# Fourteen matmul products of a feed-forward layer in another order, one weight piece ahead of another, and one token tile's split on another engine

## The chip, the cores and the metric

The kernel runs on one core of one Trainium2 chip. The metric is device time in microseconds (us) of one execution. Five engines work side by side, each through its own queue in the order of the program: TensorE (PE, matmuls), VectorE (DVE), ScalarE (ACT), GpSimd (POOL), and SyncE (SP), which here only issues DMAs.

## What is computed

One layer of a bidirectional hybrid backbone over 128 context tokens and 1024 latent tokens, 1152 in all, with a model width of 1024. The change touches the end of the mixer and the first product of the feed-forward part:

```python
out = (g_rg * y_rg + g_ml * y_ml) @ lw['w_out']          # output projection
...
x = layer_norm(ALPHA * x + gate1 * mix, lw['ln_g'][0], lw['ln_b'][0])
u = layer_norm(x) * (1.0 + scale2) + shift2
hid = jnp.square(jax.nn.relu(u @ lw['w_fc'] + lw['b_fc']))   # 1024 -> 4096
x = layer_norm(ALPHA * x + gate2 * (hid @ lw['w_proj'] + lw['b_proj']), ...)
```

## The kernel before

**Split operands.** Every fp32 operand is held as two parts, a rounded high part and the rest. `split` (lines 66 to 68) makes them: ACT copies the value to the high part (line 67), then another engine, DVE or POOL, subtracts (line 68). A product is three matmuls per 128 rows of the inner dimension, high by high, low by high and high by low (`mm3`, lines 111 to 113).

**Output projection (`wout`, `chain`, `chain2`, `cols`).** Nine token tiles `t` of 128 tokens are projected in turn. `chain(t)` adds the residual and normalises on DVE, ACT and POOL. `cols(t - 3)` transposes a tile on PE, scales it on ACT, writes its high part into `hi` on ACT (line 1070) and `u` to HBM (`u_d`, line 1071), and returns a function that writes the low part `lo` on DVE (line 1072). In the last pass, `t = 8`, that function (for tile 5) is called behind `chain(8)`. Then the first feed-forward products run, over columns of 384 tokens: with `c = 0` (tiles 0 to 2), then `c = 1` (tiles 3 to 5), with `chain2(7)`, `chain2(8)` and `cols(6)` to `cols(8)` between them.

**First feed-forward product (`ffn1`).** The 32 blocks of hidden columns go in 16 pairs `p`. The pairs 0 to 2 are computed plainly. Beside them DVE, ACT and POOL build sums of the inputs, `Th` and `Tl`, from `u_d` (`sums`, `t_loads`). The pairs 3 to 15 use Strassen's scheme in Winograd's form: seven products in place of eight, each for two halves `s` of the tokens, so fourteen products a pass, of 12 matmuls on 288 columns each. They are numbered 1 to 7 and use the weight pieces A11 (1), S1 (5), S2 (6), S3 (7), A12 (2), A22 (4) and S4 (3). The list `steps` sets their order. It names for each the product, the half, the PSUM bank (A, B or C, one of each per half), whether the bank is begun afresh, and what follows: `keep` copies the bank's present sum to SBUF on ACT (line 1297), and later products go on adding to that bank; `out` adds a bank and a kept copy on DVE (line 1306) and then applies the ReLU on ACT (line 1131), or the ReLU straight from the bank. `end` squares on DVE (line 1311).

Two things run between the steps. `need`, after every second step, makes one more weight piece for the next pass through the generator `prep`: a `put` (ACT's high part, then the low part on POOL or, for A12, on DVE) and one DVE sum (lines 1162 to 1171). Two pieces share a tile `w`, and there are four tiles. A pass has seven pieces, so pairs of pieces fall one way in the passes with odd `p` and another way with even `p`. A piece that begins a tile waits until every product that reads the two pieces eight back has ended. `pump`, after the other steps, makes one part of `store` for the pass before (sums of `hid` on POOL, lines 1105 to 1114, and DMAs). The last pass, 15, makes no new pieces and prepares `ffn2`.

Of the kernel before, what the change touches and what calls it, by code (L numbers as in the profile page):

```python
# [9 lines left out]
F = mybir.dt.float32  # L10
R = mybir.dt.float32r
AF = mybir.ActivationFunctionType
OP = mybir.AluOpType
# [6 lines left out]
NT = 9  # L20
C = 384
# [18 lines left out]
class Kern:  # L40
# [881 lines left out]
    def branches(self, st, hrp):  # L922
        nc, I, O = self.nc, self.I, self.O
# [16 lines left out]
        for br in range(2):  # L940
# [3 lines left out]
            for d, cs in [(0, (0,)), (1, (0,)), (0, (1,)), (1, (1,)), (0, (2,)), (1, (2,))] * (1 - br) + \  # L944
# [12 lines left out]
                w, g = pair[d]  # L957
# [45 lines left out]
        def chain(t, pss):  # L1003
            x = p3.tile([128, D], F, name="xr", tag="xr", bufs=2)
            nc.sync.dma_start(x, I["x"][t])
            y = p3.tile([128, D], F, name="y", tag="y", bufs=2)
            if t == 1:
                row("g1l", self.mod_d[0][1])
            g = rows["g1l" if t else "g1c"]
            for n in range(2):  # L1010
                nc.vector.tensor_tensor(y[:, n * 512:(n + 1) * 512], pss[n], g[:, n * 512:(n + 1) * 512], OP.mult)
            nc.vector.scalar_tensor_tensor(y, x, ALPHA, y, OP.mult, OP.add)
            mv = self.ln_stats(y)
            self.normalise(y, y, mv)
            e = nc.vector if t == NT - 1 else nc.gpsimd
            e.tensor_tensor(y, y, rows["gn"], OP.mult)
            e.tensor_tensor(y, y, rows["bn"], OP.add)
            ys[t] = y
# [9 lines left out]
        def wout(t):  # L1028
            c, o = t // 3, (t % 3) * 128
            pss = []  # L1030
            for n in range(2):
                ps = self.ps.tile([128, 512], F, name="wps", tag="xb", bufs=5)
                s = slice(n * 512, (n + 1) * 512)
                for k in range(KT):
                    self.mm3(ps, mh[c][0][:, k, o:o + 128], mh[c][1][:, k, o:o + 128], wo[k][:, 0, s], wo[k][:, 1, s],
                             k == 0, k == KT - 1)
                pss.append(ps)
            lo = cols(t - 3) if t >= 3 else None
            chain(t, pss)
            if t == NT - 1:  # L1040
                lo()
                return
            if t >= 1:
                chain2(t - 1)
            if lo:
                lo()

        def cols(t, bank=self.pj):
            c, o = t // 3, (t % 3) * 128
            if t % 3 == 0:  # L1050
                h, l = self.hilo(c)
                self.hi.append(h)
                self.lo.append(l)
            z = xn.pop(t)
            u = z.rearrange("p (k t) -> p k t", t=128)
            j = 1 if t else 0
            for g in range(2):
                tp = bank()
                for i in range(4):
                    k = 4 * g + i  # L1060
                    nc.tensor.transpose(tp[:, i * 128:(i + 1) * 128], z[:, k * 128:(k + 1) * 128], self.ident)
                for i in range(4):
                    k = 4 * g + i
                    q = tp[:, i * 128:(i + 1) * 128]
                    if t >= 6 and g == 1:
                        nc.vector.tensor_scalar(u[:, k, :], q, m2[:, 1, k, j:j + 1], m2[:, 0, k, j:j + 1], OP.mult, OP.add)
                    else:
                        nc.scalar.activation(u[:, k, :], q, AF.Identity, scale=m2[:, 1, k, j:j + 1], bias=m2[:, 0, k, j:j + 1])
            h, l = self.hi[c][:, :, o:o + 128], self.lo[c][:, :, o:o + 128]
            nc.scalar.activation(h, u, AF.Copy)  # L1070
            nc.scalar.dma_start(self.u_d[:, :, t * 128:(t + 1) * 128], u)
            return lambda: nc.vector.tensor_tensor(l, u, h.bitcast(F), OP.subtract)

        self.hi, self.lo = [], []
        for t in range(NT):
# [46 lines left out]
    def ffn1(self, st):  # L1122
# [22 lines left out]
        def put(x, e):  # L1145
            if pos[1] % 2 == 0:
                pos[0] = self.ring.tile([128, 2, 1024], R, name="w", tag="w", bufs=4)
            o = (pos[1] % 2) * 512
            w = pos[0][:, :, o:o + 512]
            pos[1] += 1  # L1150
            self.split(w[:, 0], w[:, 1], x, e)
            ready.append(w)

        def prep():
            for p in range(3, 16):
                r = raw.pop(p)
                a11, a12, a21, a22 = (r[i][:, 512 * k:512 * k + 512] for i in range(2) for k in range(2))
                t = lambda: pe.tile([128, 512], F, name="S", tag="S", bufs=5)
                v, g = nc.vector, nc.gpsimd
                s1, s2, s4 = t(), t(), t()  # L1160
                put(a11, g)
                v.tensor_tensor(s1, a21, a22, OP.add)
                yield
                put(s1, g)
                v.tensor_tensor(s2, s1, a11, OP.subtract)
                yield
                put(s2, g)
                v.tensor_tensor(a21, a11, a21, OP.subtract)
                yield
                put(a21, g)  # L1170
                v.tensor_tensor(s4, a12, s2, OP.subtract)
                yield
                put(a12, v)
                load(p + 1, 0)
                yield
                put(a22, g)
                load(p + 1, 1)
                yield
                put(s4, g)
                yield  # L1180
# [82 lines left out]
        for _ in work:  # L1263
            pass

        A = {"A11": 0, "S1": 1, "S2": 2, "S3": 3, "A12": 4, "A22": 5, "S4": 6}
        pair = lambda k, j: lambda s: (B(self.X[0], k, s, j), B(self.X[1], k, s, j))
        tt = lambda i: lambda s: tuple(a[:, i, :, HN * s:HN * s + HN] for a in (Th, Tl))
        P = {1: ("A11", pair(0, 0)), 5: ("S1", tt(0)), 6: ("S2", tt(1)), 7: ("S3", tt(2)),
# [9 lines left out]
        for p in range(3, 16):  # L1279
            H = new_h()  # L1280
            base = 7 * (p - 3)
            bank = {}
            ev = {}

            def mul(n, s, b, first):
                if first:
                    bank[b, s] = self.pj()
                ps = bank[b, s][:, :HN]
                w = ready[base + A[P[n][0]]]
                xh, xl = P[n][1](s)  # L1290
                for k in range(4):
                    ks = slice(k * 128, k * 128 + 128)
                    self.mm3(ps, w[:, 0, ks], w[:, 1, ks], xh[:, k, :], xl[:, k, :], first and k == 0, k == 3, not first)

            def keep(i, s):
                ev[i, s] = pe.tile([128, HN], F, name="e", tag="e", bufs=6)
                nc.scalar.activation(ev[i, s], bank["A", s][:, :HN], AF.Copy)  # L1297

            hb = lambda i, s, j: H[:, i, 2 * HN * s + HN * j:2 * HN * s + HN * j + HN]

            def out(i, s, j, b, e=None):
                o = hb(i, s, j)
                if e is None:
                    relu(o, bank[b, s][:, :HN], 2 * p + i)
                else:
                    nc.vector.tensor_tensor(o, bank[b, s][:, :HN], ev[e, s], OP.add)
                    relu(o, o, 2 * p + i)

            def end(s):
                q = H[:, :, 2 * HN * s:2 * HN * s + 2 * HN]  # L1310
                nc.vector.tensor_tensor(q, q, q, OP.mult)

            steps = [(1, 0, "A", True, lambda: keep(1, 0)), (1, 1, "A", True, lambda: keep(1, 1)),
                     (5, 0, "C", True, None), (6, 0, "A", False, lambda: keep(2, 0)),
                     (5, 1, "C", True, None), (6, 1, "A", False, lambda: keep(2, 1)),
                     (7, 0, "A", False, lambda: (keep(3, 0), out(1, 0, 1, "C", 3))),
                     (2, 0, "B", True, lambda: out(0, 0, 0, "B", 1)),
                     (7, 1, "A", False, lambda: (keep(3, 1), out(1, 1, 1, "C", 3))),
                     (4, 0, "A", False, lambda: out(1, 0, 0, "A")),
                     (2, 1, "B", True, lambda: out(0, 1, 0, "B", 1)),  # L1320
                     (3, 0, "C", False, lambda: (out(0, 0, 1, "C", 2), end(0))),
                     (4, 1, "A", False, lambda: out(1, 1, 0, "A")),
                     (3, 1, "C", False, lambda: (out(0, 1, 1, "C", 2), end(1)))]
            for i, (n, s, b, first, after) in enumerate(steps):
                mul(n, s, b, first)
                if after:
                    after()
                if i % 2:
                    need(base + 8 + i // 2 + 1)
                else:  # L1330
                    pump()
                if p == 15:
                    early(i)
            if p < 15:
                stores.append(store(p, H))
# [431 lines left out]
```

## Time and profile before

| | us |
|---|---|
| median of 3 runs | 2231.91 (2229.61 to 2234.83) |
| the profiled execution | 2234.51 |
| its span, from the first to the last instruction | 2232.4 |
| PE busy in it | 2112.8 (95%) |
| DVE, ACT, POOL busy | 1409.6, 994.9, 854.0 |

The profiled execution lies 2.6 us above the median and within the spread of the runs. 2.1 us of it lie outside the span. The stage that the change is about runs from some 1441 to 1824 us: the last tiles of the output projection to 1447, the plain pairs to 1522, the thirteen passes to 1823. In the rows of a timeline the first number is the start in us from the span's start, the second the duration in us, and the note in brackets the idle time of that engine just before and what ended it.

### The profile page before, as it was taken

The page shows a single profiled execution, that of the slowest core. Times are in us where ns is not written, and L with a number is a line of the kernel's source. Part 1 is how long each engine was busy: PE and PEld are TensorE (multiplying, and loading weights), DVE is VectorE, ACT ScalarE, POOL GpSimd, SP SyncE. Part 2 cuts the span into 40 slices and gives each one's busy share as a digit, 9 for nine tenths or more (in the row PEclk, how much of TensorE's full clock was granted, in tenths as well). Part 3 has the DMA queues.
Part 4 walks back from the last instruction along what each step waited for, and adds up shares of the span by engine and source line. Part 5 has one row for each costly group of instructions (what it writes and reads, how often), then busy time and mean ns, then how long its engine had stood idle before and what let it go on. Part 6 is the DMA issues. An engine that isn't in the chain of part 4 may idle for free. (4 is left out here: it accounts for less than half of the span.)

```text
span 2232.4 us, 31968 instructions
## 1 busy us (share of the span) xinstructions
PE 2112.8 (95%) x12507; PEld 1986.1 (89%) x12507; DVE 1409.6 (63%) x2248; ACT 994.9 (45%) x1634; POOL 854.0 (38%) x507
## 2 busy tenths in 40 slices
PE   7999999999999999999989999999999998999984
PEld 3889999999999989999989998899999996888863
DVE  4456776676675644888564656866454556566677
ACT  5455425414424525777721423655444443343333
POOL 1402213312421312332212214448566656466476
PEclk9999999999999999999989999999999999999997
DMA  7121241142122141110533333454343464342532
GB/s 275 38 71 50 66 146 64 54 133 86 62 87 83 53 77 46 48 48 29 165 120 128 118 117 115 131 199 136 125 143 121 147 245 158 136 170 79 204 118 108
DMA packets 116647, 251.13 MB, mean 112 GB/s; under 512 B 21332, under 2 KB 53716, under 8 KB 111888
## 3 DMA queue, kind: packets, MB, share of 16 engines
q1 hardware_dynamic: 94976, 231.19, 30.7%
q10 hardware_dynamic: 21520, 17.90, 2.4%
q8 instruction: 98, 1.61, 0.3%
q14 instruction: 53, 0.43, 0.1%
HBM read 186.38 MB, written 62.67 MB: 112 GB/s over the span
## 5 line engine op out<-in xcount | busy, mean ns | idle before, releaser
L111 PE MATMUL pj<-hi,w 128*128 128x384 f32 (+1 forms) x2144 | 712.8, 332 | 18.1 <-ACT XP L805 7.9
L112 PE MATMUL pj<-lo,w 128*128 128x384 f32 (+1 forms) x2144 | 709.8, 331 | 12.9 <-DVE lo L68 6.3
L113 PE MATMUL pj<-hi,w 128*128 128x384 f32 (+1 forms) x2144 | 709.2, 331 | 1.3 <-POOL w L68 1.1
L111 PEld LDWEIGHTS pj<-hi,w 128*128 128x128 f32 x2144 | 406.4, 190 | 20.3 <-ACT XP L805 8.2
L112 PEld LDWEIGHTS pj<-lo,w 128*128 128x128 f32 x2144 | 406.4, 190 | 15.4 <-DVE lo L68 6.9
L113 PEld LDWEIGHTS pj<-hi,w 128*128 128x128 f32 x2144 | 406.0, 189 | 1.9 <-POOL w L68 1.4
L68 POOL TENSOR_TENSOR w<-ws,w 128x512 fp32r<-128x512 f32 (+1 forms) x64 | 113.1, 1769 | 292.0 <-ACT w L67 283.8
L111 PE MATMUL pps<-w,hi 128*128 128x512 f32 x512 | 204.0, 398 | 11.3 <-ACT w L67 9.1
L112 PE MATMUL pps<-w,hi 128*128 128x512 f32 x512 | 204.0, 398 | 6.2 <-POOL w L68 4.1
L113 PE MATMUL pps<-w,lo 128*128 128x512 f32 x512 | 202.9, 396 | 1.4 <-DVE lo L68 1.4
L68 DVE TENSOR_TENSOR w<-ws,w 128x1024 fp32r<-128x1024 f32 (+1 forms) x85 | 112.7, 1334 | 122.6 <-ACT w L67 122.5
L67 ACT ACTIVATE w<-ws 128x1024 fp32r<-128x1024 f32 (+1 forms) x149 | 129.5, 878 | 80.8 <-PE pj L113 67.5
L467 POOL PARTITION_ALL_REDUCE aacc<-aacc x16 | 56.0, 3541 | 256.6 <-DVE aacc L466 256.6
L722 POOL TENSOR_TENSOR CS<-Cst,CS 128x516 fp32r<-128x516 f32 x56 | 73.8, 1319 | 158.2 <-ACT CS L721 147.7
L111 PE MATMUL pj<-Th,w 128*128 128x288 f32 x416 | 123.3, 296 | 8.0 <-ACT e L1297 8.0
L111 PEld LDWEIGHTS pps<-w,hi 128*128 128x128 f32 x512 | 98.0, 191 | 34.5 <-ACT w L67 10.4
L112 PEld LDWEIGHTS pps<-w,hi 128*128 128x128 f32 x512 | 98.0, 191 | 29.7 <-POOL w L68 4.9
L113 PE MATMUL pj<-Th,w 128*128 128x288 f32 x416 | 122.6, 295 | 0.0
L112 PE MATMUL pj<-Tl,w 128*128 128x288 f32 x416 | 122.5, 295 | 0.0
L113 PEld LDWEIGHTS pps<-w,lo 128*128 128x128 f32 x512 | 98.1, 192 | 23.4 <-DVE lo L68 1.9
L68 POOL TENSOR_TENSOR lo<-lo,hi 128x1024 fp32r<-128x1024 f32 (+1 forms) x31 | 84.8, 2735 | 74.0 <-ACT hi L67 74.0
L67 ACT ACTIVATE w<-raw 128x512 fp32r<-128x512 f32 x88 | 50.9, 622 | 109.9 <-issue 62.8
(348 smaller groups left out, 4493.2 us busy)
## 6 DMA issues: line engine op xcount, KB each, us to landing
ws<-in_w_in SPq DMA_DIRECT2D x56, 512.0 KB
lo<-h_d SPq DMA_DIRECT2D x28, 1024.0 KB
aw<-in_w_ada SPq DMA_DIRECT2D x64, 256.0 KB
ws<-in_w_fc SPq DMA_DIRECT2D x32, 512.0 KB
h_d<-Hf SPq DMA_DIRECT2D x32, 512.0 KB
raw<-in_w_pr SPq DMA_DIRECT2D x32, 512.0 KB
h_d<-S SPq DMA_DIRECT2D x48, 256.0 KB
gm<-gs ACTq DMA_DIRECT2D x48, 192.0 KB
```

The costliest lines, as they stand in the source:

```text
L67: self.nc.scalar.activation(hi, x, AF.Copy)
L68: (eng or self.nc.vector).tensor_tensor(lo, x, hi.bitcast(F), OP.subtract)
L111: mm(out, lhsT=ah, rhs=bh, start=first, stop=False, skip_group_check=onto)
L112: mm(out, lhsT=ah, rhs=bl, start=False, stop=False, skip_group_check=onto)
L113: mm(out, lhsT=al, rhs=bh, start=False, stop=last, skip_group_check=onto)
L467: nc.gpsimd.partition_all_reduce(acc[j], acc[j], channels=128, reduce_op=ReduceOp.add)
L722: nc.gpsimd.tensor_tensor(CS[d][1], Cst[d], CS[d][0].bitcast(F), OP.subtract)
```

## The change

Four edits. The order of the fourteen products is another one; the piece A12 takes place 3 in a pass and S3 place 4, both where they are made and where they are looked up; the low part of token tile 5 is made on POOL; and in the last pass of the output projection it is issued ahead of `chain(8)` and not behind it.

```diff
             lo = cols(t - 3) if t >= 3 else None
+            if t == NT - 1:
+                lo()
             chain(t, pss)
             if t == NT - 1:
-                lo()
                 return
...
-            return lambda: nc.vector.tensor_tensor(l, u, h.bitcast(F), OP.subtract)
+            e = nc.gpsimd if t == 5 else nc.vector
+            return lambda: e.tensor_tensor(l, u, h.bitcast(F), OP.subtract)
...
-                put(a21, g)
+                put(a12, v)
                 v.tensor_tensor(s4, a12, s2, OP.subtract)
                 yield
-                put(a12, v)
+                put(a21, g)
                 load(p + 1, 0)
...
-        A = {"A11": 0, "S1": 1, "S2": 2, "S3": 3, "A12": 4, "A22": 5, "S4": 6}
+        A = {"A11": 0, "S1": 1, "S2": 2, "S3": 4, "A12": 3, "A22": 5, "S4": 6}
...
-                     (5, 0, "C", True, None), (6, 0, "A", False, lambda: keep(2, 0)),
-                     (5, 1, "C", True, None), (6, 1, "A", False, lambda: keep(2, 1)),
+                     (5, 0, "C", True, None), (5, 1, "C", True, None),
+                     (6, 0, "A", False, lambda: keep(2, 0)), (6, 1, "A", False, lambda: keep(2, 1)),
+                     (2, 0, "B", True, lambda: out(0, 0, 0, "B", 1)),
                      (7, 0, "A", False, lambda: (keep(3, 0), out(1, 0, 1, "C", 3))),
-                     (2, 0, "B", True, lambda: out(0, 0, 0, "B", 1)),
+                     (2, 1, "B", True, lambda: out(0, 1, 0, "B", 1)),
                      (7, 1, "A", False, lambda: (keep(3, 1), out(1, 1, 1, "C", 3))),
                      (4, 0, "A", False, lambda: out(1, 0, 0, "A")),
-                     (2, 1, "B", True, lambda: out(0, 1, 0, "B", 1)),
                      (3, 0, "C", False, lambda: (out(0, 0, 1, "C", 2), end(0))),
```

In tables, with a product written as number and half, the order of a pass is

```
before  1.0 1.1 5.0 6.0 5.1 6.1 7.0 2.0 7.1 4.0 2.1 3.0 4.1 3.1
after   1.0 1.1 5.0 5.1 6.0 6.1 2.0 7.0 2.1 7.1 4.0 3.0 4.1 3.1
```

ACT in the middle of pass 5, from the second piece of tile w_14803 on, before the change (e_14885 is the copy kept of product 7's first half, from bank pj_14769; w_14869 takes over the tile whose pieces are S2 and S3 of this pass):

```order
L67 ACTIVATE w_14803<-S_14763 128x512
L1297 ACTIVATE e_14867<-pj_14788 128x288
L67 ACTIVATE w_14869<-ws_14698 128x512
L1297 ACTIVATE e_14885<-pj_14769 128x288
L1131 ACTIVATE Hf_14768<-Hf_14768,pack_118 128x288 x2
L67 ACTIVATE w_14869<-ws_14664 128x512
L1297 ACTIVATE e_14922<-pj_14788 128x288
```

The same place after it (e_14902 is now that copy; w_14869 takes over the tile whose pieces are S2 and A12):

```order
L67 ACTIVATE w_14803<-S_14763 128x512
L1299 ACTIVATE e_14851<-pj_14769 128x288
L1299 ACTIVATE e_14867<-pj_14788 128x288
L67 ACTIVATE w_14869<-ws_14664 128x512
L1133 ACTIVATE Hf_14768<-Hf_14768,pack_118 128x288
L1299 ACTIVATE e_14902<-pj_14769 128x288
L1133 ACTIVATE Hf_14768<-Hf_14768,pack_118 128x288
L67 ACTIVATE w_14869<-ws_14700 128x512
```

Between the piece that begins the tile and the kept copy there now stands a ReLU of `Hf_14768`, that of product 2's first half.

DVE at the same place of pass 5, before, from the third sum (S3) on:

```order
L1168 TENSOR_TENSOR ws_14698<-ws_14664,ws_14698 128x512
L1171 TENSOR_TENSOR S_14764<-ws_14664,S_14763 128x512
L1306 TENSOR_TENSOR Hf_14768<-pj_14807,e_14885 128x288
L1306 TENSOR_TENSOR Hf_14768<-pj_14891,e_14782 128x288
L68 TENSOR_TENSOR w_14869<-ws_14664,w_14869 128x512
```

and after:

```order
L1170 TENSOR_TENSOR ws_14700<-ws_14664,ws_14700 128x512
L68 TENSOR_TENSOR w_14869<-ws_14664,w_14869 128x512
L1173 TENSOR_TENSOR S_14764<-ws_14664,S_14763 128x512
L1308 TENSOR_TENSOR Hf_14768<-pj_14873,e_14782 128x288
L1308 TENSOR_TENSOR Hf_14768<-pj_14807,e_14902 128x288
```

The low part of A12 (line 68, which reads what ACT writes) and the sum S4 now stand ahead of the addition whose result that ReLU reads.

POOL at the end of the output projection, before:

```order
L1016 TENSOR_TENSOR y_13354<-y_13354,gn_12641 128x1024
L1017 TENSOR_TENSOR y_13354<-y_13354,bn_12643 128x1024
L68 TENSOR_TENSOR w_13496<-ws_13082,w_13496 128x1024
L68 TENSOR_TENSOR w_13501<-ws_13499,w_13501 128x1024
L1212 TENSOR_TENSOR e_13776<-Tl_13741 128x288
```

and after:

```order
L1016 TENSOR_TENSOR y_13354<-y_13354,gn_12641 128x1024
L1017 TENSOR_TENSOR y_13354<-y_13354,bn_12643 128x1024
L1074 TENSOR_TENSOR lo_451<-z_13279,hi_450 128x8x128
L68 TENSOR_TENSOR w_13496<-ws_13082,w_13496 128x1024
L68 TENSOR_TENSOR w_13501<-ws_13499,w_13501 128x1024
```

The low part of tile 5 stands on POOL between `chain(7)` and two weight blocks; on DVE it is gone.

## Rows read from the trace of the kernel before

**Rows 1.** Whom PE waited for, 1520 to 1826 us: total, times, longest.
```profile
PE pj L111 <- ACT e L1297: 8.0, 8, 1.7
PE pj L113 <- POOL w L68: 1.1, 1, 1.1
```
**Rows 2.** Stretches: length, busy us (instructions) of each engine, granted clock, DMA, GB/s.
```profile
1447.00:1457.00 10.00, 5.83 (x27) 5.58 (x26) 9.11 (x16) 4.42 (x7) 6.54 (x2) 0.83 0.45 158
1526.00:1824.00 298.00, 290.01 (x2173) 287.99 (x2172) 143.16 (x167) 126.99 (x271) 190.60 (x131) 1.00 0.43 142
1841.00:1849.00 8.00, 5.80 (x18) 4.31 (x18) 3.16 (x6) 2.58 (x4) 1.71 (x1) 0.79 1.03 415
```
**Rows 3.** Timeline of pass 7 around its tenth product (4.0), all engines.
```profile
1631.75 0.29 PE L113 MATMUL pj<-Th,w 128*128 128x288 f32 x1
1632.08 0.63 ACT L67 ACTIVATE w<-ws 128x512 fp32r<-128x512 f32 x1 [4.34 <-PE pj L113]
1632.62 0.39 ACT L1297 ACTIVATE e<-pj 128x288 f32<-128x288 f32 x1
...
1633.06 0.40 PE L111 MATMUL pj<-Th,w 128*128 128x288 f32 x1 [1.02 <-ACT e L1297]
```
**Rows 4.** Timeline of PE: the same wait in pass 3 and in pass 13.
```profile
1541.53 0.40 PE L111 MATMUL pj<-Th,w 128*128 128x288 f32 x1 [1.02 <-ACT e L1297]
...
1770.36 0.40 PE L111 MATMUL pj<-Th,w 128*128 128x288 f32 x1 [1.02 <-ACT e L1297]
```
**Rows 5.** Timeline of pass 3: PE at product 6.0, and DVE at the sum S1.
```profile
1530.29 0.40 PE L111 MATMUL pj<-Th,w 128*128 128x288 f32 x1 [1.72 <-ACT e L1297]
...
1533.70 0.69 DVE L1162 TENSOR_TENSOR S<-ws 128x512 f32<-128x512 f32 x1 [7.68 <-DMA ws<-in_w_fc]
```
**Rows 6.** Timeline of ACT and DVE in passes 7 and 8: what follows what, uncontended.
```profile
1625.09 0.68 DVE L1171 TENSOR_TENSOR S<-ws,S 128x512 f32<-128x512 f32 x1
...
1635.80 0.44 DVE L1306 TENSOR_TENSOR Hf<-pj,e 128x288 f32<-128x288 f32 x1
...
1636.28 0.54 ACT L1131 ACTIVATE Hf<-Hf,pack 128x288 f32<-128x288 f32 x1 [0.92 <-DVE Hf L1306]
1636.72 0.48 ACT L1131 ACTIVATE Hf<-pj,pack 128x288 f32<-128x288 f32 x1
...
1658.76 0.63 ACT L67 ACTIVATE w<-ws 128x512 fp32r<-128x512 f32 x1 [3.73 <-PE pj L113]
...
1659.42 0.69 DVE L68 TENSOR_TENSOR w<-ws,w 128x512 fp32r<-128x512 f32 x1 [4.96 <-ACT w L67]
1660.03 1.18 DVE L1306 TENSOR_TENSOR Hf<-pj,e 128x288 f32<-128x288 f32 x3
```
**Rows 7.** Timeline of POOL in pass 7, and of DVE in pass 8 beside a busy POOL.
```profile
1630.20 1.28 POOL L1111 TENSOR_TENSOR Hf<-Hf 128x512 f32<-128x512 f32 x1
...
1648.71 1.78 DVE L1168 TENSOR_TENSOR ws<-ws 128x512 f32<-128x512 f32 x1
```
**Rows 8.** Timeline of the output projection's end.
```profile
1435.64 2.38 POOL L1016 TENSOR_TENSOR y<-y,gn 128x1024 f32<-128x1024 f32 x1 [4.72 <-ACT y L144]
...
1436.28 1.76 DVE L140 SCALAR_TENSOR_TENSOR mv<-mv 128x1 f32<-128x1 f32 x1
...
1442.20 1.06 ACT L1070 ACTIVATE hi<-z 128x1024 fp32r<-128x1024 f32 x1
...
1444.64 0.16 DVE L140 SCALAR_TENSOR_TENSOR mv<-mv 128x1 f32<-128x1 f32 x1
...
1448.51 3.36 DVE L1072 TENSOR_TENSOR lo<-z,hi 128x1024 fp32r<-128x1024 f32 x1
...
1451.93 0.44 PE L112 MATMUL pj<-lo,w 128*128 128x384 f32 x1 [4.17 <-DVE lo L1072]
```
**Rows 9.** Timeline of the plain pairs: DVE at the first sum, PE at pair 2.
```profile
1475.64 0.46 DVE L1212 TENSOR_TENSOR e<-Tl,Th 128x288 f32<-128x288 f32 x1 [6.96 <-DMA Th<-u_d]
...
1497.51 0.44 PE L113 MATMUL pj<-hi,w 128*128 128x384 f32 x1 [0.16 <-DVE w L68]
```

## Prediction

> **What bounds the kernel now.** I read first whom PE waited for, then the stretches, then the timeline around each wait. From 1526 to 1824 us PE is busy for 290.0 of 298.0 us at a granted clock of 1.00, while DVE, ACT and POOL are busy for 48, 43 and 64% [rows 2]. So PE sets the pace of the thirteen passes, and an edit there is worth only what it does to PE's waits. There are nine in the stretch [rows 1]: eight on an ACT copy (line 1297), 8.0 us in total, and one of 1.1 us on a weight's low part from POOL. Six of the eight are alike, 1.02 us each, in the odd passes 3 to 13 [rows 4]; one of 1.72 us is in pass 3 [rows 5]; the rest, 8.0 - 6 x 1.02 - 1.72 = 0.16 us, is the eighth.
>
> The timeline of pass 7 says what the six are [rows 3]. PE starts the last matmul of product 7.1 at 1631.75. ACT has stood for 4.34 us before a weight piece that waits for PE; it starts 0.33 us after that matmul, and only behind it comes the kept copy of product 7.0's bank. PE, which wants to add product 4.0 to that bank, starts at 1633.06. So the bank's copy is not late because its product was late: it is queued on ACT behind a piece that waits for a weight tile. S2 and S3 share that tile, and 7.1 is its last reader. In even passes this piece does not begin a tile, and PE does not wait.
>
> From pass 3 to pass 13 the wait recurs after 1770.36 - 1541.53 = 228.83 us [rows 4]: ten passes, 140 products, five waits. Each wait loses 1.31 us from start to start less one matmul's step of 0.13, so 1.18. Then (228.83 - 5 x 1.18) / 140 = 1.59 us a product, 0.13 a matmul.
>
> Ahead of this stage lies one larger wait: PE stands for 4.17 us for the low part of token tile 5, which DVE makes late, in 3.36 us [rows 8]. In the 10 us around it the clock's mean is 0.83 [rows 2].
>
> **The change, edit by edit.** *The order of the products, odd passes.* The piece that begins a tile is put at the same step as before. Its tile now holds S2 and A12, whose last reader is product 2.1; that product stands where 7.1 stood, so ACT is released at the same point of the pass. One product (7.1) lies between this point and 4.0. PE therefore reaches 4.0 at 0.13 + 1.59 = 1.72 us after the start of 2.1's last matmul.
>
> What must happen by then is read from the order of the program: on ACT the piece's high part, then a ReLU, then the kept copy; and the ReLU reads an addition on DVE that stands behind the piece's low part and the sum S4. From rows: piece starts +0.33 [rows 3]; to the low part on DVE 1659.42 - 1658.76 = 0.66; low part to the next DVE operation 1660.03 - 1659.42 = 0.61 [rows 6]; the sum S4, a like operation of 0.68 us, the same 0.61 [rows 6]; addition to ReLU 1636.28 - 1635.80 = 0.48; ReLU to the next ACT operation 0.44 [rows 6]; copy to PE 1633.06 - 1632.62 = 0.44 [rows 3]. Sum 3.57 us. PE loses 3.57 - 1.72 = 1.85 us where it lost 1.18. That is +0.67 a pass, **+3.3 us** for the passes 5 to 13.
>
> These are uncontended times. DVE takes up to 1.78 us for such a sum when POOL works beside it [rows 7]. In pass 7 POOL's store work ended at 1631.5 [rows 7], and after the change one low part moves out of the queue ahead of it, so POOL should be idle from 1632.7, when the chain reaches DVE. I take the uncontended value. With both DVE operations at 1.78 it would be 2 x 1.1 more a pass, +11 in all.
>
> *Even passes.* The piece A12 begins no tile, but it stands in the same chain behind one that does and is released by 6.1. Counted from 6.1's last matmul: piece +0.33, 0.54 to the next ACT operation [rows 3], two copies of at most 0.44, then A12: it starts by 1.75. Its low part starts 0.66 later, at 2.41. Here POOL is busy and each DVE operation can take 1.7 us: 5.8. Then 0.48 + 0.44 + 0.44 give 7.2. Four products lie between, so PE is there at 0.13 + 4 x 1.59 = 6.5. Bounds: 0 and 0.7 a pass. With one of the two operations contended the sum is 6.1 and nothing is lost; I take 0.
>
> *Pass 3.* At 6.0 the bank now has one product more of cover: 1.72 us idle, with 0.16 more from start to start (1.18 against 1.02), is 1.88; less 1.59 leaves 0.3. At 7.0 the copy now stands behind a second weight piece, whose sum follows data that land at 1533.70 [rows 5]: two DVE operations (0.78 + 0.69), 0.03, 0.54 and 0.44 give 1536.18. PE, off from 6.0 at 1530.29, is there three products later at 1535.1: 1.1 lost against 0.3 before. At 4.0 POOL has a backlog; bounds 1.85 and 1.85 + 2.2 = 4.0. I take 3.4, with one operation fully contended and one partly. Sum: 0.3 + 1.1 + 3.4 = 4.8 against 1.88 + 0.3 + 1.18 = 3.4: **+1.4 us**, bounds -0.2 and +2.
>
> *The low part of tile 5 on POOL, ahead of chain(8).* ACT's high part ends at 1443.3 [rows 8]. POOL is idle there and takes 2.38 us for an operation of this size [rows 8]: the part is there at 1445.7, before PE asks for it behind 1447.3. The 4.17 us go. What is late next? DVE is free 3.36 us earlier for the normalising of tiles 7 and 8. But POOL's work is not free for DVE: a one-element operation of line 140 took 1.76 us beside POOL's 2.38 us, and ends with it [rows 8]. The one at 1444.64 took 0.16 alone; now it ends at 1445.7, 1.1 us later, and everything behind it. A second one, at tile 8's normalising, meets POOL's weight blocks: 0.4 by estimate. So the chain of tiles 7 and 8 moves ahead by 3.3 - 1.1 - 0.4 = 1.8 us.
>
> PE gains more than that at first, but gives it back: the last tile's `u` goes to HBM and comes back for the sums, DVE starts on them when these data land (1475.64), and from there DVE, ACT and POOL are the late ones: PE waits for DVE's weight at 1497.51 [rows 9] and for POOL's at the start of pass 3 [rows 1]. A PE that arrives earlier waits longer there. **-1.8 us**, bounds -0.5 and -4.2 (all of the wait).
>
> *Sum.* +3.3 + 0 + 1.4 - 1.8 = +2.9 us. On the profiled execution 2234.5 + 2.9 = 2237.4; that execution lay 2.6 above the median, so on the median's scale 2231.9 + 2.9 = **2234.8 us**. Its own range: -4.2 + 3.3 - 0.2 = -1.1 to -0.5 + 3.3 + 2 + 4.2 (even passes) = +9.0, so 2230.8 to 2240.9.
>
> **Rivals.** *The loop's waits go.* If the copies run ahead of the piece (if the tile is free earlier than 2.1's end, or DVE's work is done before), PE loses nothing in the odd passes: 6 x 1.18 + 1.88 + 0.3 = 9.3 gained, and 1.8: 2220.8 us. For it: six waits of one length are one cause, and two products now lie between. Against it: the wait is for a weight tile, not for the product, and the order of the program puts more between piece and copy. 0.12.
>
> *PE keeps its gain from tile 5.* If the sums are not the late ones, 4.17 + 0.2 and the slow stretch behind count, about 5: 2231.9 + 4.7 - 5 = 2231.6. 0.10.
>
> *POOL and DVE collide in the even passes too* (slower). If both DVE operations are contended, 0.7 a pass from pass 4 to 14, +4.2, and the odd passes as forecast: 2239.0. It decides when the low part of A12 is ready before POOL has drained its store work. 0.12.
>
> *The clock falls.* Behind an idle stretch of PE of 2.2 us or more rows show less than the full clock: means of 0.83 over 10 us and 0.79 over 8 us [rows 2], which is 3.4 us at the lower of the two levels (1.2 against 2.4 GHz), so 1.7 us lost each time. Six waits of 1.85 us would cost six times 1.7: 2234.8 + 10.2 = 2245. Against it: the 1.72 us idle in pass 3 [rows 5] left the clock at 1.00 [rows 2]. 0.08. The Trainium skill (TensorE: Matmul & The Clock Gate, A second HAM failure mode: psum-queue depth-cycling) says that a kernel that cycles through PSUM banks with small idle gaps can swing between the two levels; by that rule this rival is the likely one, while the six waits in the trace do not bear it out.
>
> **How the numbers follow.** Two runs of this kernel differ by about 0.2%, 4.5 us, so less counts as no change. The forecast gets 0.58; within it +2.9 with bounds -1.1 and +9.0 is above +4.5 in about a quarter, so 0.43 same and 0.15 slower. The rival of tile 5 adds 0.10 to same, the collision 0.11 and the clock 0.08 to slower, 0.01 of the collision to same, the vanished waits 0.12 to faster. Faster 0.12, same 0.54, slower 0.34. The range leaves out the vanished waits and most of the clock: 2228 to 2241.
>
> **What would show it.** In the timeline of an odd pass: ACT's piece 0.33 us after the last matmul of 2.1, DVE's low part, sum and addition behind it, then ReLU, copy and PE, with some 1.7 us of idle PE where 1.02 stood; in even passes no wait at 4.0. In pass 3 a short wait at 6.0 and longer ones at 7.0 and 4.0. At 1447 us no wait on the low part, a wait at the transposes of tile 7, a longer one than 0.16 us at the weights of pair 2, and pass 3 some 1.8 us earlier. Wrong it would be if PE does not wait at 4.0 in odd passes, or if pass 3 begins 4 us earlier.

## Result and the profile after

The changed kernel takes 2243.1 us, median of five runs (2241.6 to 2250.7), beside 2233.3 us of the kernel before: a ratio of 1.0054, 95% interval [1.0033, 1.0075]. It is slower, and above the range of the forecast, which ended at 2241. The profiled execution is the longest of the five: span 2248.9 us against 2232.4, mean granted clock 0.975 against 0.981.

Whom PE waits for in the thirteen passes, 1526 to 1842 us of the kernel after (total, times, longest), as in [rows 1]:

```profile
PE pj L111 <- ACT e L1299: 13.6, 9, 3.0
```

It is the same wait on ACT's kept copies as before, 13.6 us where 8.0 stood. The timeline of pass 7 around product 4.0 is the counterpart of [rows 3]:

```profile
1638.89 0.29 PE L113 MATMUL pj<-hi,w 128*128 128x288 f32 x1
...
1639.28 0.63 ACT L67 ACTIVATE w<-ws 128x512 fp32r<-128x512 f32 x1 [4.33 <-PE pj L113]
...
1639.94 0.69 DVE L68 TENSOR_TENSOR w<-ws,w 128x512 fp32r<-128x512 f32 x1 [7.70 <-ACT w L67]
...
1640.49 0.29 PE L113 MATMUL pj<-Th,w 128*128 128x288 f32 x1
1640.55 0.69 DVE L1173 TENSOR_TENSOR S<-ws,S 128x512 f32<-128x512 f32 x1
1641.15 0.45 DVE L1308 TENSOR_TENSOR Hf<-pj,e 128x288 f32<-128x288 f32 x1
1641.69 0.53 ACT L1133 ACTIVATE Hf<-Hf,pack 128x288 f32<-128x288 f32 x1 [1.78 <-DVE Hf L1308]
1642.13 0.39 ACT L1299 ACTIVATE e<-pj 128x288 f32<-128x288 f32 x1
...
1642.57 0.41 PE L111 MATMUL pj<-Th,w 128*128 128x288 f32 x1 [1.79 <-ACT e L1299]
```

The last matmul of product 2.1 starts at 1638.89 and ACT's piece 0.39 us later, and the chain of piece, low part, sum, addition, ReLU and copy runs as the forecast wrote it: 3.68 us from there to PE, 3.57 forecast. PE's step there is 2.08 us, so 1.95 are lost where 1.18 were.

What the forecast's sum did not have comes behind the wait. Stretches of the kernel after, as in [rows 2] (the five busy times are those of PE, of its weight loads, which overlap its matmuls, of DVE, ACT and POOL): the whole of the passes, then three of 4 us each around and behind the wait of pass 7, then 8 us around and behind the one in pass 3:

```profile
1527.00:1838.00 311.00, 297.41 (x2152) 295.31 (x2151) 147.12 (x163) 125.00 (x268) 194.96 (x130) 0.96 0.41 134
1640.00:1644.00 4.00, 2.21 (x15) 1.97 (x15) 2.42 (x5) 1.79 (x4) 0.00 (x0) 0.94 0.47 96
1644.00:1648.00 4.00, 4.00 (x22) 4.00 (x22) 0.85 (x2) 1.36 (x4) 1.28 (x1) 0.63 0.44 168
1648.00:1652.00 4.00, 4.00 (x32) 4.00 (x31) 1.32 (x2) 2.35 (x5) 1.99 (x2) 1.00 0.00 0
1544.00:1552.00 8.00, 6.83 (x30) 6.83 (x31) 1.99 (x5) 3.14 (x7) 1.28 (x1) 0.57 0.45 131
```

Before, the clock of these passes was 1.00 [rows 2]. Now it is 0.63 in the 4 us behind the wait: PE is busy all the time and gets through 22 matmuls where 32 pass at 1.00. The same fall stands in all six odd passes from 3 to 13; in the even passes there is none.

**Where the 16.5 us of the two profiled spans lie**, read between the same instructions in both traces. Up to a step of PE in the output projection ahead of every changed instruction (1437.3 before, 1440.3 after) the profiled execution of after was already 2.95 us late, by chance: the twelve profiles of this document run the same program up to that step and reach it between 1435.9 and 1440.5 us. From there to product 5.0 of pass 3 it took 87.6 us instead of 89.5: -1.9. Pass 3 from 5.0 to its last product: 24.9 instead of 21.2, +3.8. Even passes: 22.24 and 22.24. Odd passes 5 to 13: two passes take 48.07 instead of 45.77, five times +2.30. Pass 15: +1.0. Behind the passes: -0.9, less than the profiles of like programs differ there (407.1 to 409.6 us in all twelve, before being the longest). Sum 2.95 - 1.9 + 3.8 + 11.5 + 1.0 - 0.9 = 16.5. Without the chance of the start, 13.5 us are the change's in this execution. Between the medians lie 9.8.

### The profile page after: what moved, and what is told of

It reads as the page before. It is cut to its first block, busy times and chain, and to the rows that moved or that the text cites. A ratio compares the mean times of both kernels' runs of the same rounds, so it can differ in the third digit from the quotient of the medians.

```text
span 2248.9 us, 31968 instructions
## 1 busy us (share of the span) xinstructions
PE 2125.6 (95%) x12507; PEld 1997.4 (89%) x12507; DVE 1416.8 (63%) x2247; ACT 994.0 (44%) x1634; POOL 860.4 (38%) x508
## 5 line engine op out<-in xcount | busy, mean ns | idle before, releaser
L112 PEld LDWEIGHTS pj<-lo,w 128*128 128x128 f32 x2144 | 408.4, 190 | 10.4 <-DVE lo L68 6.9
L111 PE MATMUL pj<-Th,w 128*128 128x288 f32 x416 | 126.0, 303 | 13.6 <-ACT e L1299 13.6
L113 PE MATMUL pj<-Th,w 128*128 128x288 f32 x416 | 125.3, 301 | 0.0
```

Of the source, the lines that this page charges most:

```text
L111: mm(out, lhsT=ah, rhs=bh, start=first, stop=False, skip_group_check=onto)
L112: mm(out, lhsT=ah, rhs=bl, start=False, stop=False, skip_group_check=onto)
L113: mm(out, lhsT=al, rhs=bh, start=False, stop=last, skip_group_check=onto)
```

## Experiments

The theory after the result: PE's 1.79 us of idle time at 4.0 is ACT's queue, as forecast, and an idle stretch of that length makes the clock fall, in any order of the products. The rivals: the new order of the products and their banks lets the clock fall by itself; or the edits on tile 5 are the cause. (Each half of the tokens has its own bank, so both orders change the bank with every product.)

### Each half of the change alone

`loop_alone` is the changed kernel with the output projection as before:

```
-            if t == NT - 1:
-                lo()
             chain(t, pss)
             if t == NT - 1:
+                lo()
                 return
...
-            e = nc.gpsimd if t == 5 else nc.vector
-            return lambda: e.tensor_tensor(l, u, h.bitcast(F), OP.subtract)
+            return lambda: nc.vector.tensor_tensor(l, u, h.bitcast(F), OP.subtract)
```

> The loop edits alone (new order of the products, A12's piece ahead of S3's); the out-projection as before. Theory: the 1.95 us that PE stands at product 4.0 in odd passes, and the lower clock that follows some of these waits, belong to the loop. Then pass 3 starts where it did before (1522.4), five waits with a step of 2.0 to 2.1 us stand in the passes 5 to 13, the clock is below 1.00 behind some of them, and the time is 5 to 16 us above the kernel before. Rival: the clock falls because the out-projection edits have moved the stage or changed what runs ahead of it; then the waits are there but the clock holds at 1.00 behind them, and the time is +5 us at most (five times 0.8 and 1 to 2 in pass 3).

Measured: 2246.3 us beside 2234.2, ratio 1.0054 [1.0041, 1.0066]. The waits are the same (13.7 us, nine), and the clock falls in pass 3 and behind four of the five waits of the passes 5 to 13. Two stretches each, around and behind the waits of pass 5 and of pass 13:

```profile
1592.00:1596.00 4.00, 2.21 (x15) 1.97 (x14) 2.10 (x5) 2.11 (x5) 0.15 (x1) 0.92 0.52 114
1596.00:1600.00 4.00, 4.00 (x23) 4.00 (x21) 0.91 (x2) 1.03 (x3) 1.13 (x1) 0.65 0.42 155
1784.00:1788.00 4.00, 2.21 (x17) 1.98 (x16) 2.38 (x5) 1.83 (x5) 0.00 (x0) 1.00 0.46 99
1788.00:1792.00 4.00, 4.00 (x32) 4.00 (x32) 0.92 (x2) 1.64 (x5) 1.30 (x1) 1.00 0.43 163
```

The last of these waits is as long as the others (a step of 2.08 us), and the clock holds. That gives the price: two passes take 48.07 us with the fall and 46.54 without it, so one fall costs 1.53 us and the longer wait itself 46.54 - 45.77 = 0.77. The loss belongs to the loop.

`tile5_alone` is the other half, on the kernel before (the same lines, the other way round).

> The out-projection edits alone (low part of token tile 5 on POOL, ahead of chain(8)); the loop as before. Theory: PE's wait of 4.17 us goes, but the token sums are not earlier and pass 3 starts 1.1 us later as in the changed kernel: 0 to +1.5 us, waits of 1.02 us in the odd passes as before, clock 1.00 in the loop. Rival (the forecast's step): the chain of tiles 7 and 8 is 1.8 us earlier and pass 3 with it: -1.8 us.

Measured: 2232.1 us beside 2234.2, ratio 0.9996 [0.9987, 1.0005]. Both expectations are half right. PE's wait on the low part is gone, and 5.0 of pass 3 comes 1.0 us earlier, counted from the same step of the output projection. But product 6.0 waits for a copy that stands on ACT behind a weight piece, and that piece for data that land no earlier than before. The piece before and in `tile5_alone`, then PE at 6.0:

```profile
1529.31 0.63 ACT L67 ACTIVATE w<-ws 128x512 fp32r<-128x512 f32 x1 [3.41 <-DMA ws<-in_w_fc]
```

```profile
1529.65 0.63 ACT L67 ACTIVATE w<-ws 128x512 fp32r<-128x512 f32 x1 [3.91 <-DMA ws<-in_w_fc]
...
1530.63 0.61 PE L111 MATMUL pj<-Th,w 128*128 128x288 f32 x1 [2.88 <-ACT e L1299]
```

```profile
1528.00:1536.00 8.00, 5.37 (x29) 5.37 (x30) 2.59 (x4) 1.56 (x4) 4.51 (x4) 0.79 0.69 234
```

The idle time there is 2.88 us instead of 1.72 [rows 5], the clock falls to a mean of 0.79 over these 8 us (the last fence: the stretch as in [rows 2]), and the gain is spent.

### The wait made longer in the old order

`before_act1` and `before_act2` put one or two ACT copies behind the waiting piece; the products stand as before (the line for two):

```
                 if i % 2:
                     need(base + 8 + i // 2 + 1)
+                    if i == 5 and p % 2 and p < 15:
+                        for _ in range(2):
+                            nc.scalar.activation(ev[1, 0], ev[1, 0], AF.Copy)
```

> The kernel before with one more ACT copy (a kept tile onto itself, 288 elements) behind the waiting weight piece in the odd passes: the same wait in the old order, longer by 0.44 us. Theory (the clock falls by the length of PE's wait alone): 1.46 us lost instead of 1.02 to 1.18 plus 0.44, a step of about 1.75 us, which lies between the 1.31 that leaves the clock and the 2.08 after which it mostly falls; if the clock holds, +0.44 x 6 = +2.6 us. Rival (the falls belong to the new order of the products): the clock holds for any of these lengths.

> The kernel before with two such copies: the wait in the old order as long as in the changed kernel, a step of about 2.2 us. Theory: behind most of the six waits the clock falls for some us as in the changed kernel, 0.9 + 1.5 a pass, +9 to +14 us. Rival (the falls belong to the new order of the products): the clock stays at 1.00 and the time is +5.3 us.

Measured: one copy makes the idle time 1.35 us, the clock stays at 1.00 in all of the passes, ratio 1.0006 [0.9996, 1.0015] (0.33 us six times is 2.0). Two copies make it 1.82, and the time goes to 1.0054 [1.0039, 1.0069], as in the changed kernel. The passes of the first, then four stretches of the second, around and behind the waits of pass 5 and of pass 7:

```profile
1527.00:1822.00 295.00, 285.04 (x2140) 283.18 (x2139) 140.60 (x163) 127.63 (x274) 187.46 (x130) 1.00 0.43 140
```

```profile
1592.00:1596.00 4.00, 2.18 (x14) 1.95 (x14) 0.82 (x2) 2.31 (x6) 2.68 (x3) 0.91 0.01 2
1596.00:1600.00 4.00, 4.00 (x23) 4.00 (x23) 1.17 (x3) 2.09 (x5) 0.30 (x1) 0.67 0.36 72
1640.00:1644.00 4.00, 2.17 (x16) 1.94 (x15) 0.82 (x2) 2.19 (x6) 2.69 (x3) 1.00 0.00 0
1644.00:1648.00 4.00, 4.00 (x32) 4.00 (x31) 1.52 (x3) 2.22 (x6) 0.44 (x1) 1.00 0.31 59
```

The order of the products is not the cause: in the old one the clock falls behind four of the five long waits of the passes 5 to 13 too. And it is not every wait: behind that of pass 7, of the same 1.82 us, it holds here. What tells the two apart was not tested.

### The new order without the exchange of the pieces

`order_alone` has the new list of products, with S3's piece ahead of A12's:

```
-        A = {"A11": 0, "S1": 1, "S2": 2, "S3": 4, "A12": 3, "A22": 5, "S4": 6}
+        A = {"A11": 0, "S1": 1, "S2": 2, "S3": 3, "A12": 4, "A22": 5, "S4": 6}
...
-                put(a12, v)
+                put(a21, g)
                 v.tensor_tensor(s4, a12, s2, OP.subtract)
                 yield
-                put(a21, g)
+                put(a12, v)
```

> The new order of the fourteen products alone; the pieces in the old order (S3's ahead of A12's), the out-projection as before. The tile of S2 and S3 is now read last by product 7.1, right ahead of 4.0. From ACT's queue: piece 0.33, 0.54 to the ReLU, 0.44 to the copy, 0.44 to PE, less 0.13: 1.6 us lost, a step of 1.75, DVE not in the chain. Theory: about +0.5 a pass where the clock holds, +2 to +3 us, and the same waits as with one more copy in the old order. Rival (the exchange of A12 and S3 is what made the wait, and two products between users of a bank remove it): no wait, -7 us.

Measured: ratio 1.0022 [1.0012, 1.0032]. The chain is the one expected, to within two hundredths:

```profile
1634.77 0.29 PE L113 MATMUL pj<-Th,w 128*128 128x288 f32 x1
1635.10 0.63 ACT L67 ACTIVATE w<-ws 128x512 fp32r<-128x512 f32 x1 [5.87 <-PE pj L113]
1635.63 0.52 ACT L1131 ACTIVATE Hf<-Hf,pack 128x288 f32<-128x288 f32 x1
...
1636.06 0.39 ACT L1297 ACTIVATE e<-pj 128x288 f32<-128x288 f32 x1
...
1636.50 0.40 PE L111 MATMUL pj<-Th,w 128*128 128x288 f32 x1 [1.44 <-ACT e L1297]
```

A step of 1.73 where 1.75 was worked out, and the clock at 1.00 throughout the passes. The time, 2239.5 us beside 2234.7, is above the 2 to 3 us expected: a second, short wait at 4.1 (a step of 0.52, so 0.39 a pass) and one of a like kind in pass 15 (a step of 1.05) were not in it. Putting two products between users of a bank does not remove the wait, since the wait is not for the bank's product.

### The low part of A12 on POOL

`loop_pool` is `loop_alone` with one letter changed:

```
-                put(a12, v)
+                put(a12, g)
```

> The loop edits, with the low part of A12 on POOL instead of DVE; the out-projection as before. Theory: DVE's low part and the sum behind it leave the chain; what is left is piece 0.33, 0.54 to the ReLU, 0.44 to the copy, 0.44 to PE = 1.75 us against the 1.72 us that PE takes to 4.0: nearly no wait in the odd passes, clock 1.00, -5 to -8 us against the kernel before. Rival (the wait is not DVE's part of the chain but the piece and the tile): 1.3 us or more stays.

Measured: 2227.8 us beside 2234.7, ratio 0.9970 [0.9959, 0.9981]. An odd pass takes 22.42 us where an even one takes 22.24, the clock is 1.00. So DVE's low part and the sum behind it were the part of the chain that made it longer than the cover.

### The copy ahead of the piece

`after_late` and `before_late` are the two kernels with the weight piece of step 5 (counted from 0) asked for behind step 7, together with the one of that step, so that the kept copy of 7.0's bank stands ahead of the waiting piece on ACT; products and weights are untouched. The expectations speak of two pieces; behind step 5 each pass asks for one.

```
                 if i % 2:
-                    need(base + 8 + i // 2 + 1)
+                    if i != 5:
+                        need(base + 8 + i // 2 + 1)
```

> The changed kernel, with the two weight pieces that were asked for behind step 5 asked for behind step 7, so that on ACT the kept copy of product 7.0's bank stands ahead of the piece that waits for a weight tile. Theory (the copy is late only because it is queued behind that piece, and the clock falls only because of that wait): no wait in the odd passes, clock 1.00 throughout, two passes in 44.5 us where the changed kernel has 48.1 and the one before 45.8; against the kernel before 6 times 1.2 gained, 1 to 3 lost ahead of and in pass 3: about -5 us. Rival: the order that changes banks with every product lets the clock fall by itself; then the clock stays under 1.00 in places with no wait, and the time is above the kernel before.

> The kernel before, with the same two pieces asked for behind step 7 instead of step 5: the kept copy of product 7.0's bank stands ahead of the waiting piece on ACT, in the old order of the products. Theory (the six waits of 1.02 us are the ACT queue's, not the order of the products): they go without any new order, two passes in 44.5 us, about -7 us. Rival: the bank's copy is bound by the product itself, since only one product lies between 7.0 and 4.0 in the row; then some 0.5 to 1 us stays in each odd pass, and the same appears in even passes.

Measured, on one chip: `after_late` 2222.9 us, 0.9948 [0.9935, 0.9962]; `before_late` 2223.0 us, 0.9952 [0.9939, 0.9964]. In both, every pass from 4 to 14 takes 22.24 us and PE has no wait in it; the passes of `after_late`, then of `before_late`:

```profile
1526.00:1812.00 286.00, 284.36 (x2143) 283.63 (x2143) 145.35 (x163) 127.66 (x268) 188.27 (x129) 1.00 0.44 146
```

```profile
1530.00:1817.00 287.00, 285.26 (x2153) 284.82 (x2152) 146.00 (x164) 127.21 (x269) 190.85 (x131) 1.00 0.44 146
```

Both beat the kernel before by 11 us, and neither new order nor exchange is needed for it: one skipped request is. From 5.0 of pass 3 to the end of the passes `before_late` gains 7.9 us, 1.29 in each of five odd passes and 1.4 in pass 3; another 2.6 us between the two profiles lie in the stage behind. They need not be the edit's: `before_act1`, whose program there is that of before, takes 407.2 us for that stage, before 409.6 and `before_late` 407.1. So 7.9 of the 11 us are explained and the rest is open.

With and without the edits on tile 5:

> The loop edits with the two pieces asked for behind step 7, the out-projection as before: the kernel after_late without the edits on token tile 5. Theory (the tile-5 edits are worth 1 to 2 us at the start of pass 3, as read in three profiles): 1 to 2 us above the 2222.9 us of after_late, no wait in the odd passes. Rival (they are worth nothing by the end, since PE waits for pair 2's weights and at product 6.0 instead): the same time as after_late.

> The old order of the products with the pieces asked for behind step 7, and the edits on token tile 5: the kernel before_late with these edits. Theory: 1 to 2 us below the 2223.0 us of before_late, less what a longer wait at product 6.0 of pass 3 gives back (a step of 3.2 us there and a lower clock behind it in tile5_alone): 0 to -2 us. Rival: the same as before_late or slower, if the clock falls behind product 6.0 of pass 3.

Measured: `loop_late` 0.9966 [0.9952, 0.9979], `tile5_late` 0.9965 [0.9953, 0.9978]. In the old order the rival came: 6.0 waits with a step of 3.2 us and the clock falls behind it, so the edits give nothing over `before_late` (378.5 us from the same step of the output projection to the end of the passes, against 377.6). In the new order 6.0 has one product more of cover, and `after_late` with the edits lies below `loop_late` without them (0.9948 against 0.9966), on different chips and with intervals that overlap. Between the same two instructions the profiles take 377.0 and 378.5 us: a gain of 1 to 2 us there is likely, from one profile of each, and the times do not show it.

### All of it in one table

Idle time of PE at 4.0 in the passes 5 to 13, and what the clock did behind it:

| kernel | order | idle, us | clock fell | two passes, us | ratio |
|---|---|---|---|---|---|
| before | old | 1.02 | 0 of 5 | 45.77 | 1 |
| before_act1 | old | 1.35 | 0 of 5 | 46.09 | 1.0006 |
| order_alone | new | 1.44 | 0 of 5 | 46.67 | 1.0022 |
| after | new | 1.79 | 5 of 5 | 48.07 | 1.0054 |
| loop_alone | new | 1.79 | 4 of 5 | 48.07; without 46.54 | 1.0054 |
| before_act2 | old | 1.82 | 4 of 5 | 48.1; without 46.6 | 1.0054 |
| loop_pool | new | 0 | 0 of 5 | 44.66 | 0.9970 |
| before_late | old | 0 | 0 of 5 | 44.48 | 0.9952 |
| after_late | new | 0 | 0 of 5 | 44.48 | 0.9948 |

## Why the prediction was wrong, step by step

**Odd passes: right in mechanism and size.** 1.85 us lost at 4.0 were forecast, 1.95 measured; +0.67 a pass forecast, +0.77 measured. The chain had every link that the forecast named, in its order, and the DVE operations ran uncontended (0.69 each). `loop_pool` and `after_late` confirm it from the other side: take DVE out, or the copy out of the queue, and the wait goes.

**Even passes: right.** No wait, 22.24 us a pass as before, and in the way that the forecast took: one of the two DVE operations was slow beside POOL. In pass 6 the last matmul of 6.1 starts at 1611.90 and 4.0 at 1618.38; the copy was there half a microsecond before PE needed it:

```profile
1614.78 1.78 DVE L1173 TENSOR_TENSOR S<-ws,S 128x512 f32<-128x512 f32 x1
...
1617.45 0.39 ACT L1299 ACTIVATE e<-pj 128x288 f32<-128x288 f32 x1
```

**Pass 3: right in kind, the size a little high.** 0.3, 1.1 and 3.4 us were forecast at 6.0, 7.0 and 4.0. Measured are 0.4, 0.9 and 3.1 us lost; against 3.4 before that is +1.0 instead of +1.4. At 4.0 one of the two DVE operations was slow beside POOL, as taken:

```profile
1541.63 1.71 POOL L1116 TENSOR_TENSOR S<-Hf,S 128x512 f32<-128x512 f32 x1
...
1542.14 1.75 DVE L1173 TENSOR_TENSOR S<-ws,S 128x512 f32<-128x512 f32 x1
...
1545.17 0.61 PE L111 MATMUL pj<-Th,w 128*128 128x288 f32 x1 [2.96 <-ACT e L1299]
```

**Tile 5: right in the path, and in size where the clock held.** -1.8 forecast, -1.9 in the changed kernel's profile, -1.0 in `tile5_alone`. POOL's operation, the 1.10 us of the one-element operation beside it and the new waits at tile 7's transposes and at pair 2 came as written; the rows answer to [rows 8, 9]:

```profile
1446.35 2.39 POOL L1074 TENSOR_TENSOR lo<-z,hi 128x1024 fp32r<-128x1024 f32 x1 [1.90 <-ACT hi L1071]
```

```profile
1447.66 1.10 DVE L140 SCALAR_TENSOR_TENSOR mv<-mv 128x1 f32<-128x1 f32 x1
```

```profile
1456.21 1.09 PE L1062 MATMUL xb<-ident,z 128*128 128x128 f32 x8 [1.50 <-ACT z L144]
```

```profile
1498.59 0.44 PE L113 MATMUL pj<-hi,w 128*128 128x384 f32 x1 [2.59 <-DVE w L68]
```

```profile
1496.00:1504.00 8.00, 5.41 (x31) 5.41 (x32) 7.68 (x9) 4.02 (x9) 5.94 (x6) 1.00 0.50 135
```

The last fence is the stretch around that wait: the clock holds. In `tile5_alone` it falls behind the same wait:

```profile
1496.62 0.69 PE L113 MATMUL pj<-hi,w 128*128 128x384 f32 x1 [2.61 <-DVE w L68]
```

```profile
1494.00:1502.00 8.00, 5.39 (x23) 5.38 (x23) 7.67 (x9) 4.04 (x9) 5.95 (x6) 0.79 0.48 127
```

It falls there in `after_late` and `tile5_late` too. From the step of the output projection to 5.0 of pass 3 the eight profiles without the tile-5 edits take 89.5 to 89.9 us; the four with them take 87.6 (after), 88.0, 88.5 and 88.7. The forecast's size is that of the one in which the clock held.

The sign that the prediction named for it, pass 3 some 1.8 us earlier, can't be read from the absolute times, because that execution was 2.95 us late already; it has to be counted from an instruction ahead of the change.

**Not in the sum:** a step of 1.05 us at 4.1 in pass 15. The ReLU ahead of its kept copy waits for an addition that stands on DVE behind a weight part of the next stage; it costs +1.0:

```profile
1833.23 2.47 DVE L68 TENSOR_TENSOR w<-ws,w 128x512 fp32r<-128x512 f32 x1 [2.07 <-ACT w L67]
1835.63 0.45 DVE L1308 TENSOR_TENSOR Hf<-pj,e 128x288 f32<-128x288 f32 x1
...
1836.99 0.40 PE L111 MATMUL pj<-Th,w 128*128 128x288 f32 x1 [0.76 <-ACT e L1299]
```

**The step that failed is the clock.** The forecast's sum has no term for it, since the longest wait in the passes before had left it at 1.00. Waits alone come to 1.0 + 5 x 0.77 - 1.9 + 1.0 - 0.9 = +3.0 us, where the forecast's sum was +2.9; the +1.0 of pass 15 and the -0.9 behind the passes were not in it, and that they cancel is luck. On top lie five falls at 1.53 us and one of 3.8 - 1.0 = 2.8 in pass 3: 10.4 us. The prediction had this as a rival at 2245 us, with 1.7 us a fall and a chance of 0.08. Price and time were good; the chance was not. It rested on one row, an idle time of 1.72 us in pass 3 that left the clock at 1.00 [rows 5, 2]. The prediction sets it beside waits of 1.85 us, but that is the time lost, 0.16 more than the idle time: 1.69 us of idle time were forecast and 1.79 measured. So the waits of the passes 5 to 13 were forecast just below the longest that had left the clock alone, and came out just above it. For pass 3 the prediction's own numbers called for a fall: 3.4 us lost at 4.0 lie beyond the 2.2 us of idle time behind which it reads a lower clock, and yet no fall is in that term. It measured 2.8.

One row says little there. In the passes of all twelve profiles idle stretches up to 1.74 us never lowered the clock, and of the 22 from 1.79 us up 19 did. But length alone does not decide it: two waits of 1.79 and 1.82 us are among the three that did not, and the third is the longer 1.97 us at 6.0 of pass 3 in `loop_pool`:

```profile
1531.09 0.40 PE L111 MATMUL pj<-Th,w 128*128 128x288 f32 x1 [1.97 <-ACT e L1297]
```

```profile
1530.00:1538.00 8.00, 6.91 (x51) 6.87 (x52) 4.06 (x5) 3.09 (x7) 6.22 (x5) 1.00 0.56 180
```

With a forecast wait that close to the longest one seen at full clock, and six times over, this case deserved a share like that of the forecast itself. How many falls the median run had is not known: the five runs spread from 2241.6 to 2250.7 us, the mean clock from 0.981 in the shortest to 0.975 in the longest, which would fit fewer falls in the shorter ones, and only the longest was profiled.

Two smaller slips of the prediction change nothing here. The terms of the rival on tile 5 (4.17, 0.2 and 0.17 x 10 for the slow stretch) add up to 6.1 and not to "about 5". And on the two collisions at tile 5, put at 1.1 and 0.4 us, the first one-element operation took 0.94 us longer (1.10 instead of 0.16) and the second 0.15 (0.31 instead of 0.16).

The Trainium skill (TensorE: Matmul & The Clock Gate, A second HAM failure mode: psum-queue depth-cycling) describes such falls in a kernel that cycles through PSUM banks and leaves small idle gaps between groups of matmuls. The runs here part the two halves of that: both orders change the bank with every product, and both run at a clock of 1.00 once the wait is gone (`after_late`, `before_late`); the old order loses the clock when its wait is lengthened (`before_act2`). What tells here is the idle gap, not the change of banks.

## What to carry to other kernels

A wait that recurs on one engine can be a queue's order and not a late product: ask what stands ahead of the late instruction on its own engine, and move the request for that, before moving the work of the engine that waits. A PE wait that grows costs its own growth only as long as the clock holds: when a change lengthens a recurring wait close to or past the longest one that the trace shows without a fall, price each with and without a fall, and keep both in the range.

## What the runs showed of the hardware

- In a stream of matmuls that is otherwise gapless, idle stretches of PE of 1.02, 1.35 and 1.44 us left the granted clock at 1.00 in every odd pass (before, `before_act1`, `order_alone`); 1.79 to 1.83 us lowered it, to the lower of the two levels (a matmul every 0.24 us instead of 0.13), in 13 of 15 waits of the passes 5 to 13. In the passes no fall stands apart from such a stretch.
- A longer idle stretch is not sure to lower it. Where the stage behind the passes begins, PE stands for 2.2 us in the old order and 2.5 us in the new; the clock fell there in 7 of 12 profiles, in before [rows 2, third line] and not in `before_late`:

```profile
1839.63 0.50 PE L111 MATMUL pps<-w,hi 128*128 128x512 f32 x1 [2.19 <-DVE C L1556]
```

```profile
1838.00:1846.00 8.00, 6.37 (x28) 5.27 (x29) 2.87 (x4) 2.01 (x2) 2.48 (x2) 1.00 1.03 409
```

- Such a fall costs 1.53 us in the passes, twice the 0.77 us by which the wait had grown. Behind the 2.96 us of idle time in pass 3 it cost about 2.8.
- The same wait of the same kernel does or does not bring a fall from pass to pass. Where it does in the passes 5 to 13, the fall began between 0.1 and 1.3 us after PE had started again; in pass 3 of the changed kernel it began 0.6 us before. What decides it was not found. The five waits of one execution are not five independent cases: in the changed kernel the time from PE's start to the fall shrinks from wait to wait, from 1.26 to 0.12 us.
